# The even mixer in another order: attention pairs spread over inverse and chain, column groups at once, whole inverse steps

## Chip, core and metric

The kernel runs on one core of a Trainium2 chip. The metric is the time of one execution on the device in microseconds (us). Before the change the median of three runs is 1186.69 us (1185.93 to 1187.33).

## What is computed

One inference step of a two-layer trunk of width 1024, for 256 prompt tokens and 8 sample tokens that share the weights (264 columns in all). Each layer is a half-step SwiGLU, a mixer and another half-step SwiGLU, with a layer norm behind each. The even layer's mixer, the only part in question here, has 8 stick-breaking attention heads and 8 RWKV-7 heads, cut from the reference:

```python
def even_mixer(h, past_k, past_v, wkv0, shift0, prm, i):
    proj = h @ prm['w_in_even'][i]
    q, k, v = (heads(c) for c in jnp.split(proj[..., :SB_COLS], 3, axis=-1))
    ...
    pb = proj[..., SB_COLS:]
    pm = pb + prm['mu_shift'][i] * (prev - pb)
    r, kr, vr, wd, ad, gd = jnp.split(pm, RWKV_SPLITS, axis=-1)
    z_w = prm['w0'][i] + jnp.tanh(wd) @ prm['w_w2'][i]
    decay = jnp.exp(-jnp.exp(-jax.nn.softplus(-z_w) - 0.5))
    iclr = jax.nn.sigmoid(prm['a0'][i] + ad @ prm['w_a2'][i])
    gate = jax.nn.sigmoid(gd) @ prm['w_g2'][i]
    ...
    out = jnp.concatenate([o_sb, o_rwkv], axis=-1) @ prm['w_out_even'][i]
```

Attention takes z = q k'/8 + bias, and weights exp(log sigmoid(z) + the reversed running sum of log sigmoid(-z)) under the causal mask. The recurrence of a head keeps a 64x64 state s with s = s w - (s kk)(kk a)' + v k' and y = s r. The sample tokens attend to 256 past positions each, in a paged cache (16 pages of 128 positions).

## The kernel before

Activations lie with their channels on the partitions and the 264 tokens along the row. Weights stream from memory in the order of use, in chunks of eight 128x128 blocks (`Stream`); ScalarE rounds each chunk to `wh` (L197) and VectorE forms the rest `wl` (L198). `block` (L288 on) makes three matmuls of 264 columns of a weight block: `wh` with the high part of the activations, `wh` with the low one, `wl` with the high one (L295 to L297).

The even mixer (`_even`) first runs six blocks of columns at once into six PSUM banks (`FIRST_IN`: decay and learning-rate ranks, four blocks of `kr`, the gate's rank), on unnormalized activations, and then corrects and evicts them (`fix`, `in_proj`). `rwkv_first` makes the small decay and rate products (`pz`, `pa`), and `rwkv_prep` is a generator that prepares one pair of RWKV heads at a time on VectorE and ScalarE: the norm of the key (`pn`, `rsqrt`), the running decay (`cs`), and the scaled operands `ar`, `K`, `B`. Beside it run the blocks of `r` (`NEXT_IN`), then query, `vr`, key and value (`LAST_IN`). `proj` makes one such block of 128 columns from eight weight blocks into a bank `pi` of a group of two banks, and yields after every two.

The recurrence is solved in chunks of 64 tokens. `gram` makes masked products of the operands; `rwkv_inverse` inverts the unit-triangular matrices of 8 heads x 4 chunks (16 pairs) in six levels, each with the products `pP`, `pX` and `pXT`, each product in two halves of sixteen 64x64 matmuls on opposite quarters of the array; `rwkv_chain` then goes over the four chunks (`pW`, `pU`, `pS`, `pY`), and `rwkv_out` normalizes and gates.

All else is interleaved by generators: `_even` steps through the inverse and then the chain, and at each yield calls `next` on `side` (`other_half`: the remaining `proj` blocks, then attention, then the first half of the output projection `po`), on `tokens` (transposes), on `samples` (the paged attention of the sample tokens: keys on VectorE, then values as `pso` on TensorE) and on `states` (the samples' RWKV state on VectorE). `self.stage` tells how far `side` is. `behind` and `issue_after` fix parts of the order; the rest of each engine's order is set when the program is built. Banks lie in four groups, A (2), B (3), C (1) and D (2), that `banks` gives names.

Of the kernel before, what the change touches and what calls it, by code (L numbers as in the profile page):

```python
# [14 lines left out]
ALU = mybir.AluOpType  # L15
# [102 lines left out]
def even_order():  # L118
    o = [("w_in_even", 0, k, m) for k in range(KD) for m in FIRST_IN]
    o += [("w_in_even", 0, k, m) for m in NEXT_IN + LAST_IN for k in range(KD)]  # L120
# [98 lines left out]
class Trunk:  # L219
# [383 lines left out]
    def _even(self, ctx, ln_in, ln_out):  # L603
# [42 lines left out]
        ps = [self.ps([128, NO], f"raw{i}", t) for i, t in enumerate(("rk", "rk", "rk", "at", "at", "mm"))]  # L646
# [9 lines left out]
        self.rwkv_first(lora, hv)  # L656
        prep = self.rwkv_prep(hv, bone)
        next(prep)
        self.r_t = self.slot([128, 4, NT], "r_t")
        for mb in NEXT_IN:  # L660
            next(prep, None)
            for _ in self.proj(mb):
                pass
        for _ in prep:
            pass
# [4 lines left out]
        self.vtok = vv[:, 1]  # L670
        self.g2 = g2
# [16 lines left out]
        while self.stage < 3:  # L688
# [34 lines left out]
    def other_half(self, bone, sbb, idb, nmb):  # L723
# [3 lines left out]
        for mb in LAST_IN[:4]:  # L727
            yield from self.proj(mb)
        self.stage = 1
        for mb in LAST_IN[4:12]:  # L730
            yield from self.proj(mb)
            if mb == LAST_IN[7]:
                self.stage = 2
        nc.sync.dma_start(out=a["shift_out"], in_=self.sh_out)
        nc.sync.dma_start(out=a["kv_out"][:, 0], in_=self.k_t)
        self.stage = 3
# [42 lines left out]
    def rwkv_first(self, lora, hv):  # L779
# [3 lines left out]
        wa = self.tmp([128, NT], "wa")  # L783
        nc.scalar.activation(wa[0:64], self.wda[0:64], AF.Tanh)
        nc.vector.tensor_copy(wa[64:128], self.wda[64:128])
        nc.scalar.activation(self.gd, self.gd, AF.Tanh, scale=0.5)
        nc.vector.tensor_scalar(out=self.gd, in0=self.gd, scalar1=0.5, scalar2=0.5, op0=ALU.mult, op1=ALU.add)
# [8 lines left out]
        with self.tc.issue_after(last.ins):  # L796
            self.tables = self.load_exp_ln()

    def rsqrt(self, o, x):

        nc = self.nc
        with self.tc.issue_after(self.tables.ins):
            nc.scalar.activation(o, x, AF.Ln)
            nc.scalar.activation(o, o, AF.Exp, scale=-0.5)
        nc.vector.scalar_tensor_tensor(out=x, in0=x, scalar=-0.5, in1=o, op0=ALU.mult, op1=ALU.mult)
        nc.vector.tensor_tensor(out=x, in0=x, in1=o, op=ALU.mult)
        nc.vector.scalar_tensor_tensor(out=o, in0=x, scalar=1.5, in1=o, op0=ALU.add, op1=ALU.mult)

    def rwkv_prep(self, hv, bone):
# [14 lines left out]
        for m in range(4):  # L824
# [98 lines left out]
    def rwkv_inverse(self):  # L923
# [18 lines left out]
        for lv in range(6):  # L942
            lm = cst[:, None, C_LVL + 64 * lv:C_LVL + 64 * lv + 64].to_broadcast([128, 8, 64])
            P = {}
            for i, s in enumerate(S):
# [10 lines left out]
                yield  # L956
            if lv == 0:
                continue
            for i, s in enumerate(S):
                if lv < 5:  # L960
# [3 lines left out]
                    yield  # L964
# [3 lines left out]
                yield  # L968
# [108 lines left out]
    def attention(self, sbb, idb, nmb):  # L1077
# [8 lines left out]
        def scores(h):  # L1086
            m, H = h // 2, slice(h % 2 * 64, h % 2 * 64 + 64)
            z = self.ps([128, 384], "z", "at")
            mm(z[:, 0:256], lhsT=self.k_t[H, m, 0:128], rhs=self.q_t[H, m, 0:256], start=True, stop=False)
            mm(z[:, 0:256], lhsT=idb, rhs=nmb, start=False, stop=True)  # L1090
            mm(z[:, 256:384], lhsT=self.k_t[H, m, 128:256], rhs=self.q_t[H, m, 128:256], start=True, stop=False)
            mm(z[:, 256:384], lhsT=idb, rhs=nmb[:, 0:128], start=False, stop=True)
            zb[h], sp[h] = att("zb"), att("sp")
            nc.scalar.activation(zb[h], z, AF.Identity, bias=sbb[:, h:h + 1])
            self.softplus(sp[h], zb[h])
# [8 lines left out]
        def values(h):  # L1104
            m, H = h // 2, slice(h % 2 * 64, h % 2 * 64 + 64)
            po = self.ps([128, NP], "pov", "at")
            w = zb[h]
            mm(po[H, :], lhsT=vtok[:, 0, h * 64:h * 64 + 64], rhs=w[:, 0:256], start=True, stop=False)
            mm(po[H, 128:256], lhsT=vtok[:, 1, h * 64:h * 64 + 64], rhs=w[:, 256:384], start=False, stop=True)
            nc.scalar.copy(self.q_t[H, m, :NP], po[H])  # L1110
# [7 lines left out]
        for h in range(10):  # L1118
# [829 lines left out]
```

## Time and profile before

| | |
|---|---|
| median of three runs | 1186.69 us |
| the profiled execution: its own time | 1181.86 us |
| its span, first to last instruction | 1180.1 us |
| TensorE busy | 1126.4 us, 95% |
| VectorE busy | 881.6 us, 75% |
| ScalarE busy | 590.8 us, 50% |
| GpSimd busy | 176.8 us, 15% |
| mean granted TensorE clock | 0.982 |

Busy times are of one execution, and a busy TensorE is not TensorE at its peak: matmuls are pipelined and their ends are modelled. So the time of a piece of its queue is read from one start to the next. The page shows the share of each engine in 40 slices, and the waits, the timeline and the stretches of single engines come from the trace. The even mixer takes some 225 us, about from 235 to 460 us.

### The profile page before, as it was taken

How to read it: one execution, taken by the hardware profiler on the slowest of the kernel's cores; microseconds unless marked ns; L12 is line 12 of the kernel's file. 1: busy time of each engine (PE TensorE's matmuls, PEld its weight loads, DVE VectorE, ACT ScalarE, POOL GpSimd, SP SyncE). 2: the span in 40 equal slices, each digit the busy share in tenths (PEclk: the TensorE clock that was granted, in tenths of full speed). 3: DMA queues.
4: the chain of work that ended last, by engine and by line, in shares of the span. 5: the costliest groups of instructions: out<-in, count | busy, mean ns of one | idle time of the engine just before them, and what ended most of it. 6: DMA issues, size and time to landing. Idle time of an engine off the chain costs nothing. (4 is left out here: it accounts for less than half of the span.)

```text
span 1180.1 us, 26369 instructions
## 1 busy us (share of the span) xinstructions
PE 1126.4 (95%) x10711; PEld 1067.7 (90%) x10711; DVE 881.6 (75%) x1739; ACT 590.8 (50%) x1030; POOL 176.8 (15%) x296
## 2 busy tenths in 40 slices
PE   7999999979999998999999999999969999999996
PEld 6999999977986677999999999999958899999995
DVE  4999855889875769988876797675669699555564
ACT  4544544664245565744454564454463366444442
POOL 0000000364535314010110112100020002000000
PEclk9999999989999999999999999999979999999998
DMA  7755656624565314476775567665564253655651
GB/s 250 234 168 157 211 177 207 205 89 123 158 184 151 124 53 143 135 240 215 262 233 174 156 201 228 203 182 178 175 200 154 86 192 116 208 180 182 183 178 49
DMA packets 66122, 204.96 MB, mean 174 GB/s; under 512 B 13464, under 2 KB 16616, under 8 KB 65744
## 3 DMA queue, kind: packets, MB, share of 16 engines
q1 hardware_dynamic: 56400, 174.09, 47.4%
q0 software_dynamic: 6560, 23.27, 6.2%
q10 hardware_dynamic: 3040, 5.92, 1.6%
q8 instruction: 84, 1.38, 0.5%
q14 instruction: 38, 0.31, 0.1%
HBM read 192.22 MB, written 10.86 MB: 172 GB/s over the span
## 5 line engine op out<-in xcount | busy, mean ns | idle before, releaser
L198 DVE TENSOR_TENSOR wl<-raw,wh 128x1024 fp32r<-128x1024 f32 (+2 forms) x317 | 388.5, 1227 | 184.0 <-ACT wh L197 180.9
L197 ACT CAST wh<-raw 128x1024 fp32r<-128x1024 f32 (+2 forms) x317 | 329.9, 1041 | 344.5 <-issue 100.0
L295 PE MATMUL pd<-hh,wh 128*128 128x264 f32 x704 | 200.8, 285 | 0.0
L297 PE MATMUL pd<-hh,wl 128*128 128x264 f32 x704 | 200.7, 285 | 0.0
L296 PE MATMUL pd<-hl,wh 128*128 128x264 f32 x704 | 199.1, 283 | 0.0
L295 PE MATMUL pg<-xh,wh 128*128 128x264 f32 x648 | 184.8, 285 | 3.3 <-DVE fixc L467 1.8
L297 PE MATMUL pg<-xh,wl 128*128 128x264 f32 x648 | 184.4, 285 | 1.6 <-DVE wl L198 1.5
L296 PE MATMUL pg<-xl,wh 128*128 128x264 f32 x648 | 183.6, 284 | 0.0
L297 PE MATMUL pu<-xh,wl 128*128 128x264 f32 x608 | 173.2, 285 | 2.0 <-DVE wl L198 1.9
L295 PE MATMUL pu<-xh,wh 128*128 128x264 f32 x608 | 172.9, 284 | 0.0
L296 PE MATMUL pu<-xl,wh 128*128 128x264 f32 x608 | 172.7, 284 | 0.0
L295 PEld LDWEIGHTS pd<-hh,wh 128*128 128x128 f32 x704 | 132.4, 188 | 0.6
L297 PEld LDWEIGHTS pd<-hh,wl 128*128 128x128 f32 x704 | 132.6, 188 | 0.2
L296 PEld LDWEIGHTS pd<-hl,wh 128*128 128x128 f32 x704 | 132.4, 188 | 0.0
L295 PEld LDWEIGHTS pg<-xh,wh 128*128 128x128 f32 x648 | 122.4, 189 | 4.2 <-ACT xh L451 2.0
L297 PEld LDWEIGHTS pg<-xh,wl 128*128 128x128 f32 x648 | 121.8, 188 | 2.7 <-DVE wl L198 2.7
L296 PEld LDWEIGHTS pg<-xl,wh 128*128 128x128 f32 x648 | 122.5, 189 | 0.0
L297 PEld LDWEIGHTS pu<-xh,wl 128*128 128x128 f32 x608 | 114.3, 188 | 3.0 <-DVE wl L198 2.9
L296 PEld LDWEIGHTS pu<-xl,wh 128*128 128x128 f32 x608 | 115.0, 189 | 0.0
L295 PEld LDWEIGHTS pu<-xh,wh 128*128 128x128 f32 x608 | 114.9, 189 | 0.0
L295 PE MATMUL raw<-rh,wh 128*128 128x266 f32 x192 | 56.7, 295 | 3.8 <-DVE r L346 3.7
L498 ACT CAST hh<-h 128x264 fp32r<-128x264 f32 x79 | 32.2, 409 | 55.6 <-DVE h L497 55.4
(559 smaller groups left out, 2214.6 us busy)
## 6 DMA issues: line engine op xcount, KB each, us to landing
raw<-in_w SPq DMA_DIRECT2D x308, 512.0 KB, 3.7
raw<-in_w SPq DMA_DIRECT2D x7, 384.0 KB, 5.5
gxd<-gc SPq DMA_DIRECT2D x8, 256.0 KB, 2.7
qb<-qd POOLq DMA_DIRECT2D x8, 256.0 KB, 4.5
FT<-wd POOLq DMA_DIRECT2D x8, 256.0 KB, 5.4
bF<-in_bF POOLq DMA_DIRECT2D x8, 256.0 KB, 4.4
rot<-rotd ACTq DMA_DIRECT2D x5, 384.0 KB, 5.2
rotd<-T POOLq DMA_DIRECT2D x2, 768.0 KB
```

The lines of the kernel that those rows point to most:

```text
L197: nc.scalar.copy(wh[:, :w], raw[:, :w])
L198: nc.vector.tensor_tensor(out=wl[:, :w], in0=raw[:, :w], in1=wh[:, :w], op=ALU.subtract)
L295: mm(ps, lhsT=wh, rhs=xh, start=start, stop=False)
L296: mm(ps, lhsT=wh, rhs=xl, start=False, stop=False)
L297: self.last_mm = mm(ps, lhsT=wl, rhs=xh, start=False, stop=stop)
L498: self.last = [nc.scalar.copy(hh[:, m, :], h), self.last_mm]
```

## The change

Query blocks come right behind the first six (`SOON_IN`) and between the receptance blocks; key, value and `vr` blocks are taken by `attention` itself, which now goes by pairs of heads and starts with the inverse. A pair's scores use both halves of the rows, its values both halves of the columns. The samples' values run four pages at a time on four groups of 32 columns, so the pages are loaded four at a time. `rwkv_inverse` yields once per product and no longer per half. In the preparation five operations go from VectorE to ScalarE or GpSimd, and `rsqrt` has one VectorE operation less and a square on ScalarE. The table load for exponential and logarithm stands behind the last hyperbolic tangent, and `softplus` behind that load. The core of the diff:

```diff
-FIRST_IN = [WDA, WKR, WKR + 1, WKR + 2, WKR + 3, WGD]
-NEXT_IN = [WR + i for i in range(4)]
-LAST_IN = list(range(4)) + [WVR + i for i in range(4)] + list(range(4, 12))
+FIRST_IN = [WDA, WGD, WKR, WKR + 1, WKR + 2, WKR + 3]
+SOON_IN = [WQ, WQ + 1]
+NEXT_IN = [WR, WQ + 2, WR + 1, WQ + 3, WR + 2, WR + 3]
+LAST_IN = [WK, WV, WVR, WVR + 1, WK + 1, WV + 1, WVR + 2, WVR + 3, WK + 2, WV + 2, WK + 3, WV + 3]
...
-        ps = [self.ps([128, NO], f"raw{i}", t) for i, t in enumerate(("rk", "rk", "rk", "at", "at", "mm"))]
+        ps = [self.ps([128, NO], f"raw{i}", t) for i, t in enumerate(("rk", "rk", "rk", "at", "at", "sa"))]
...
         for i, _ in enumerate(self.rwkv_inverse()):
-            if self.stage < 3:
+            for _ in range(1 + i % 2):
                 next(side)
-            if i < BURST:
-                next(side)
-            if i >= 4 and i % 3 == 2:
+            if i >= 4:
                 next(tokens, None)
-            if i > 5 and (i % 2 or i > 24):
                 next(samples, None)
...
         for i, _ in enumerate(self.rwkv_chain(bone)):
             next(gate, None)
-            next(side, None)
-            next(side, None)
+            for _ in range(1 + i % 2):
+                next(side, None)
...
-        nc.vector.scalar_tensor_tensor(out=x, in0=x, scalar=-0.5, in1=o, op0=ALU.mult, op1=ALU.mult)
-        nc.vector.tensor_tensor(out=x, in0=x, in1=o, op=ALU.mult)
+            nc.scalar.activation(s, o, AF.Square)
+        nc.vector.scalar_tensor_tensor(out=x, in0=x, scalar=-0.5, in1=s, op0=ALU.mult, op1=ALU.mult)
...
-            nc.vector.tensor_scalar(out=lw, in0=lw, scalar1=1.0, scalar2=None, op0=ALU.add)
+            nc.scalar.activation(lw, lw, AF.Copy, bias=1.0)
...
-            nc.vector.tensor_scalar(out=kki, in0=ti, scalar1=0.5, scalar2=0.5, op0=ALU.mult, op1=ALU.add)
+            nc.scalar.activation(kki, ti, AF.Copy, scale=0.5, bias=0.5)
...
-            nc.vector.tensor_scalar(out=kf, in0=ti, scalar1=hv[:, 8 + m:9 + m], scalar2=hv[:, 12 + m:13 + m],
-                                    op0=ALU.mult, op1=ALU.add)
+            nc.scalar.activation(kf, ti, AF.Identity, scale=hv[:, 8 + m:9 + m], bias=hv[:, 12 + m:13 + m])
...
+        def scores(m):
+            z = [self.ps([128, 384], "z", "at") for _ in range(2)]
+            for o, k, q, n in ((slice(0, 256), slice(0, 128), slice(0, 256), nmb),
+                               (slice(256, 384), slice(128, 256), slice(128, 256), nmb[:, 0:128])):
+                for i in range(2):
+                    H = slice(64 * i, 64 * i + 64)
+                    mm(z[i][:, o], lhsT=self.k_t[H, m, k], rhs=self.q_t[H, m, q], start=True, stop=False)
+                for i in range(2):
+                    mm(z[i][:, o], lhsT=idb, rhs=n, start=False, stop=True)
...
+        def values(m):
             po = self.ps([128, NP], "pov", "at")
+            for w in range(2):
+                for i in range(2):
+                    h = 2 * m + i
+                    mm(po[64 * i:64 * i + 64, 128 * w:256], lhsT=vtok[:, w, h * 64:h * 64 + 64],
+                       rhs=zb[h][:, (0, 256)[w]:(256, 384)[w]], start=w == 0, stop=w == 1)
...
+        turns = [[8 * g + 2 * i + p for i in range(4)] for g in range(2) for p in range(2)]
+        for e in turns[0]:
             load(e)
         for g in range(2):
+            po = self.ps([128, 512], "pso", "sa")
+            for p in range(2):
+                for _ in range(4):
+                    yield
                 with self.tc.issue_after(self.anchor.ins):
+                    for i, e in enumerate(turns[2 * g + p]):
+                        mm(po[32 * i:32 * i + 32, :], lhsT=w[:, e * 8:e * 8 + 32], rhs=vp[e], start=p == 0, stop=p == 1)
+                if p == 0:
+                    for e in turns[2 * g + 1]:
+                        load(e)
```

How the order of the instructions moves is shown at three places. The first is VectorE in the opening, the preparation of the first pair of RWKV heads (`pn` is the norm, `t0` and `t1` the steps of `rsqrt`, `cs` the running decay, `wl` the splits of weight chunks). Before, and then with the change:

```order
L832 TENSOR_SCALAR t0_3379<-pn_3381 128x264
L805 SCALAR_TENSOR_TENSOR t0_3379<-t0_3379,t1_3383 128x264
L806 TENSOR_TENSOR t0_3379<-t0_3379,t1_3383 128x264
L807 SCALAR_TENSOR_TENSOR t1_3383<-t0_3379,t1_3383 128x264
L198 TENSOR_TENSOR wl_3554<-raw_3551,wh_3553 128x1024
L835 SCALAR_TENSOR_TENSOR kk_3390<-kr_t_3030,vec_76,t1_3383 128x264
L839 SCALAR_TENSOR_TENSOR cs_3393<-cst_75,lw_3343 128x264
L847 TENSOR_SCALAR kki_3399<-ti_3344 128x264
L198 TENSOR_TENSOR wl_3624<-raw_3621,wh_3623 128x1024
L848 TENSOR_TENSOR kki_3399<-kki_3399,kk_3390 128x264
L850 TENSOR_SCALAR ti_3344<-ti_3344,hv_3019 128x264
L853 TENSOR_TENSOR ar_3374<-kk_3390,E1_3370 128x4x64
```

```order
L826 TENSOR_SCALAR t0_3445<-pn_3447 128x264
L199 TENSOR_TENSOR wl_3481<-raw_3478,wh_3480 128x1024
L800 SCALAR_TENSOR_TENSOR t0_3445<-t0_3445,t2_3451 128x264
L801 SCALAR_TENSOR_TENSOR t1_3449<-t0_3445,t1_3449 128x264
L829 SCALAR_TENSOR_TENSOR kk_3457<-kr_t_3030,vec_76,t1_3449 128x264
L833 SCALAR_TENSOR_TENSOR cs_3460<-cst_75,lw_3407 128x264
L199 TENSOR_TENSOR wl_3552<-raw_3549,wh_3551 128x1024
L842 TENSOR_TENSOR kki_3466<-kki_3466,kk_3457 128x264
L846 TENSOR_TENSOR ar_3440<-kk_3457,E1_3436 128x4x64
```

One step of `rsqrt` and the two affine steps ahead of `kki` and `ti` are gone from VectorE; the addition to `lw` (L837 before) too.

The second place is TensorE at the scores (`z` the scores, `idb` and `nmb` the mask). Before, one head between weight blocks and the chain, and with the change the first pair, ahead of the first `gram`:

```order
L297 MATMUL pi_4740<-xh_3226,wl_4344 128x264
L1089 MATMUL z_5028<-qk_3667 128x256
L1090 LDWEIGHTS idb_3023
L1090 MATMUL z_5028<-nmb_3025,idb_3023 128x256
L1091 MATMUL z_5028<-qk_3667 128x128
L1092 LDWEIGHTS idb_3023
L1092 MATMUL z_5028<-nmb_3025,idb_3023 128x128
L1003 MATMUL pS_5047<-VT_4892,KT_4606 64x64 x5
```

```order
L1086 MATMUL z_3866<-qk_3338 128x256
L1086 MATMUL z_3867<-qk_3338 128x256
L1088 LDWEIGHTS idb_3023
L1088 MATMUL z_3866<-nmb_3025,idb_3023 128x256
L1088 LDWEIGHTS idb_3023
L1088 MATMUL z_3867<-nmb_3025,idb_3023 128x256
L1086 MATMUL z_3866<-qk_3338 128x128
L1086 MATMUL z_3867<-qk_3338 128x128
```

The two heads' matmuls of one kind now stand next to each other, and the first pair stands ahead of the inverse.

The third place is the end of the mixer, TensorE just ahead of the output projection (`pso` the samples' values, `pst` their transposition, `pov` the heads' values, `po` the output projection). Before, and with the change:

```order
L1209 MATMUL pso<-vp,sw 32x512
L1099 MATMUL pcs<-att,cst 128x384
L1100 MATMUL pcs<-att,cst 128x128
L996 MATMUL pU<-Wn,XT 64x64 x3
L1108 MATMUL pov<-att,vv 64x256
L1109 MATMUL pov<-att,vv 64x128
L996 MATMUL pU<-Wn,XT 64x64 x5
L1003 MATMUL pS<-VT,KT 64x64 x2
L1108 MATMUL pov<-att,vv 64x256
L1109 MATMUL pov<-att,vv 64x128
L1003 MATMUL pS<-VT,KT 64x64 x5
L1221 MATMUL pst<-cst,soc 128x128
```

```order
L1296 MATMUL psy<-cst,sys 32x32 x2
L1224 MATMUL pso<-vp,sw 32x512 x2
L1108 MATMUL pov<-att,vv 64x256 x2
L1108 MATMUL pov<-att,vv 64x128
L1224 MATMUL pso<-vp,sw 32x512
L1108 MATMUL pov<-att,vv 64x128
L1296 MATMUL psy<-cst,sys 32x32 x2
L1043 MATMUL pgm<-YT,cst 128x288
L1224 MATMUL pso<-vp,sw 32x512
L1049 MATMUL pgv<-t_5755,cst 128x288
L1237 MATMUL pst<-cst,soc 128x128
L296 MATMUL po<-xh,wh 128x264 x4
```

Before, the last `pso` stood ahead of the last chain step, and `pst` inside it; now the last four `pso` come behind that step, one by one, and `pst` is the last matmul ahead of `po`.

## Rows read from the trace of the kernel before

**Rows 1.** The page, part 1: busy us, share of the span, instructions.

```profile
PE 1126.4 (95%) x10711; PEld 1067.7 (90%) x10711; DVE 881.6 (75%) x1739; ACT 590.8 (50%) x1030; POOL 176.8 (15%) x296
```

**Rows 2.** TensorE's waits from 235 to 460 us: total, times, longest.

```profile
PE pi L295 <- DVE fixt L469: 3.8, 1, 3.8
PE pi L295 <- ACT pb L590: 2.6, 1, 2.6
PE pP L940 <- DVE ss L947: 2.3, 2, 1.5
```

**Rows 3.** Stretches: length, busy us (count) of PE, PEld, DVE, ACT, POOL; clock; DMA.

```profile
240.00:250.00 10.00, 7.75 (x29) 6.72 (x30) 8.36 (x19) 6.54 (x15) 7.08 (x19) 0.66 0.17 53
260.00:270.00 10.00, 9.03 (x60) 8.97 (x61) 8.98 (x19) 5.16 (x13) 6.86 (x18) 0.83 0.36 107
296.00:356.00 60.00, 59.88 (x1122) 52.98 (x1117) 49.24 (x78) 22.33 (x46) 26.95 (x36) 1.00 0.59 175
```

**Rows 4.** Timeline of TensorE in the inverse: start us, us, instruction, count.

```profile
297.14 1.15 PE L940 MATMUL pP<-X,ss 64*64 64x64 f32 x32
298.22 0.39 PE L295 MATMUL pi<-xh,wh 128*128 128x264 f32 x1
298.45 0.28 PE L296 MATMUL pi<-xl,wh 128*128 128x264 f32 x1
298.57 0.28 PE L297 MATMUL pi<-xh,wl 128*128 128x264 f32 x1
...
299.14 1.15 PE L940 MATMUL pP<-X,ss 64*64 64x64 f32 x32
...
344.75 1.15 PE L940 MATMUL pX<-st,XT 64*64 64x64 f32 x32
345.73 1.10 PE L940 MATMUL pXT<-XT,st 64*64 64x64 f32 x32
```

**Rows 5.** Groups of VectorE from 235 to 296 us: busy us, mean ns, idle before.

```profile
L806 DVE TENSOR_TENSOR t<-t,t 128x264 f32<-128x264 f32 x4 | 1.7, 430 | 0.1
```

**Rows 6.** Timeline of TensorE at the samples' values (two records to a matmul).

```profile
363.35 1.90 PE L1209 MATMUL pso<-vp,sw 128*32 128x512 f32 x6
...
380.73 1.91 PE L1209 MATMUL pso<-vp,sw 128*32 128x512 f32 x4
...
426.73 1.04 PE L1209 MATMUL pso<-vp,sw 128*32 128x512 f32 x2
```

**Rows 7.** Timeline of TensorE at one head's scores and another's values.

```profile
386.58 0.70 PE L1089 MATMUL z<-qk 64*128 64x256 f32 x2
387.21 0.28 PE L1090 MATMUL z<-nmb,idb 128*128 128x256 bf16 x1
387.43 0.49 PE L1091 MATMUL z<-qk 64*128 64x128 f32 x2
387.84 0.23 PE L1092 MATMUL z<-nmb,idb 128*128 128x128 bf16 x1
...
388.93 0.65 PE L1108 MATMUL pov<-att,vv 128*64 128x256 f32 x2
389.41 0.38 PE L1109 MATMUL pov<-att,vv 128*64 128x128 f32 x2
389.72 0.27 PE L1003 MATMUL pS<-VT,KT 64*64 64x64 f32 x1
```

**Rows 8.** The tile `vp`: durations in ns (least, median, most), and landing.

```profile
L1197 POOL DMA_INDIRECT vp<-in_cache_v,idx x16: 944/972/1432, 353.1 to 410.2; - x16
...
DMA to landing us min/median/max: 3.4/3.7/4.6
```

**Rows 9.** Timeline of VectorE at the samples' sums.

```profile
427.81 0.69 DVE L1214 TENSOR_TENSOR pv<-pso,cst 128x512 f32<-128x512 f32 x1 [0.71 <-PE pso L1209]
...
429.68 1.04 DVE L1216 TENSOR_REDUCE soc<-pv 128x64 f32<-128x512 f32 x1
...
432.19 0.73 DVE L1226 COPY qk<-pst 64x16 f32<-64x16 f32 x4 [1.13 <-PE pst L1221]
```

More of the change, by code (lines that the diff above doesn't have):

```diff
@@ L119, in even_order @@
     o = [("w_in_even", 0, k, m) for k in range(KD) for m in FIRST_IN]
[L120 removed]
+    o += [("w_in_even", 0, k, m) for m in SOON_IN + NEXT_IN + LAST_IN for k in range(KD)]
     o += [("w_out_even", 0, k, m) for m in range(KD) for k in range(4)]
@@ L670, in _even @@
         self.vtok = vv[:, 1]
+        for mb in SOON_IN:
+            for _ in self.proj(mb):
+                pass
+        self.rwkv_first(lora, hv)
+        prep = self.rwkv_prep(hv, bone)
+        next(prep)
+        self.r_t = self.slot([128, 4, NT], "r_t")
+        for i, mb in enumerate(NEXT_IN):
+            if i < 4:
+                next(prep)
+            for _ in self.proj(mb):
+                pass
+        for _ in prep:
+            pass
         self.g2 = g2
@@ L796, in rwkv_first @@
         with self.tc.issue_after(last.ins):
+            last = nc.scalar.activation(self.gd, self.gd, AF.Tanh, scale=0.5)
+        nc.gpsimd.tensor_scalar(out=self.gd, in0=self.gd, scalar1=0.5, scalar2=0.5, op0=ALU.mult, op1=ALU.add)
+        with self.tc.issue_after(last.ins):
             self.tables = self.load_exp_ln()
@@ L1084, in attention @@
         att = lambda name: self.tw([128, 384], "att", bufs=6)
[L1086 to L1095, printed above, removed]
+        def scores(m):
[9 more added lines that the diff above has]
+                h = 2 * m + i
+                zb[h], sp[h] = att("zb"), att("sp")
+                nc.scalar.activation(zb[h], z[i], AF.Identity, bias=sbb[:, h:h + 1])
+            for i in range(2):
+                self.softplus(sp[2 * m + i], zb[2 * m + i])
         def weights(h):
@@ L1102, in weights @@
             nc.scalar.activation(zb[h], zb[h], AF.Exp)
-        def values(h):
-            m, H = h // 2, slice(h % 2 * 64, h % 2 * 64 + 64)
+        def values(m):
             po = self.ps([128, NP], "pov", "at")
[L1107 to L1110, printed above, removed]
+            for w in range(2):
+                for i in range(2):
+                    h = 2 * m + i
+                    mm(po[64 * i:64 * i + 64, 128 * w:256], lhsT=vtok[:, w, h * 64:h * 64 + 64],
+                       rhs=zb[h][:, (0, 256)[w]:(256, 384)[w]], start=w == 0, stop=w == 1)
+            nc.scalar.copy(self.q_t[:, m, :NP], po)
         def tokens(m):
@@ L1116, in tokens, with blocks @@
             nc.scalar.copy(vtok[:, :, m * 128:m * 128 + 128], ps)
-        for h in range(10):
-            m = h // 2
-            if h in (0, 2, 4, 6):
-                yield from self.proj(WV + m)
-            if h < 8:
-                scores(h)
-            if h in (0, 2, 4, 6):
-                tokens(m)
-            if h == 6:
-                nc.sync.dma_start(out=self.a["kv_out"][:, 1], in_=self.v_t)
+        left = list(LAST_IN)
+        def blocks(n):
+            for _ in range(n):
+                yield from self.proj(left.pop(0))
+        for m in range(4):
+            yield from blocks((2, 2, 2, 0)[m])
+            if m == 0:
+                self.stage = 1
+            scores(m)
+            yield
+            tokens(m)
+            yield from blocks((1, 1, 1, 0)[m])
+            if m == 3:
+                yield
+            for i in range(2):
+                weights(2 * m + i)
+            yield
+            yield from blocks((1, 1, 1, 0)[m])
+            if m == 1:
+                self.stage = 2
+                nc.sync.dma_start(out=self.a["shift_out"], in_=self.sh_out)
+            if m == 2:
+                for i, t in enumerate((self.k_t, self.v_t)):
+                    nc.sync.dma_start(out=self.a["kv_out"][:, i], in_=t)
                 self.new_h()
                 self.oh, self.ol = self.xh, self.xl
-            if 1 <= h < 9:
-                weights(h - 1)
-            if h >= 2:
-                values(h - 2)
+            values(m)
             yield
@@ L1198, in load @@
                                          in_offset=bass.IndirectOffsetOnAxis(ap=idx[:, e:e + 1], axis=0))
[L1200 removed]
+        turns = [[8 * g + 2 * i + p for i in range(4)] for g in range(2) for p in range(2)]
+        for e in turns[0]:
             load(e)
         for g in range(2):
[L1203 to L1212 removed]
+            po = self.ps([128, 512], "pso", "sa")
+            for p in range(2):
+                for _ in range(4):
+                    yield
+                with self.tc.issue_after(self.anchor.ins):
+                    for i, e in enumerate(turns[2 * g + p]):
[3 more added lines that the diff above has]
+                        load(e)
+            if g == 0:
+                for e in turns[2]:
+                    load(e)
             t = self.page([128, 512], "pv")
```

56 lines of the change are left out of this document (12 added, 44 removed).

## The prediction

> **What bounds the kernel now.** Read first the page's busy shares: TensorE is busy for 1126.4 of 1180.1 us [rows 1], so only work that leaves TensorE's queue, or time in which it stands still, can be won. The even mixer lies between about 235 us (first `pi` block) and 460 us. Read there the stretches, then TensorE's waits. Two kinds of loss are to be seen. In the opening TensorE stands still: 3.8, 2.6 and 2.3 us, 8.7 us in all [rows 2], and the mean granted clock is 0.66 and 0.83 in two stretches of 10 us [rows 3], which is 6.8 and 3.4 us at the lower of its two levels (1.2 for 2.4 GHz). From 296 us on it never waits and the clock is at 1.00 [rows 3]: that part is as long as the instructions in TensorE's queue. There, the time of a piece is read from start to start. Outside this stretch the change touches nothing; I take the rest as it is.
>
> **How the pieces of TensorE's queue add up.** A block of six matmuls between two groups of the inverse takes 0.92 us (298.22 to 299.14), and the starts in it are 0.12 us apart, so 0.2 us of it is the change from one shape to the other. A group of sixteen 64x64 matmuls takes 1.08 us after a block (297.14 to 298.22), and 0.98 us when the next group follows at once [rows 4]. As a check I added up everything in the queue this way for 296 to 460 us, and it came to the length of that stretch within 1%.
>
> **The change, part by part.** The matmuls are the same ones, 672 of them weight blocks; what changes is their order.
>
> - *Opening.* Two query blocks (48 matmuls, 5.8 us) come ahead of the decay and gate work, query blocks alternate with receptance blocks, and the sixth first accumulator lies in a bank of its own, so that the third block no longer waits for its eviction. Both long waits of [rows 2] had this cause: the block behind found its bank not yet read, once because the read stood behind five others on VectorE, once because ScalarE's read needed a buffer that VectorE gives back. Along with it, 16 of VectorE's instructions in the preparation (four lines of four, of which the costliest takes 0.43 us each [rows 5]; some 6 us in all) go to ScalarE or vanish. They stood in the queue that TensorE waited for. ScalarE is busy for 6.5 and 5.2 of 10 us there [rows 3] and takes them in its gaps; without gaps, four of them would make each pair 1.7 us later. To be won at most: 8.7 us of waits and (6.8 - 2.25 + 3.4 - 0.97) / 2 = 3.5 us of slow clock (what TensorE stood still inside those two stretches taken off), 12.2 us. I leave 1.5 us for new short waits, since a preparation of a pair takes VectorE about ten instructions of 0.4 to 0.7 us, partly overlapped, some 4 us, and one or two weight splits, while TensorE gets 48 to 72 matmuls, 6 to 9 us, between two of them. Bounds: 0, and 9 us, as long as now.
> - *Sample values.* Sixteen matmuls of 32 columns stand in twelve places now, nine single ones of 1.0 us and three runs of 1.9 us [rows 6], 14.7 us. Four on four column groups come together now: three turns at 1.0 us, and the last turn in three places, 6.0 us. That gains **8.7 us**. That column groups run side by side is to be seen already: three matmuls of which two lie on different groups (363.35) take 1.90 us, as long as two on one group (380.73) [rows 6]. Four at once no row shows; if only two ran together, each turn but the last takes 1.9 and it is 6.0, if none, 0.
> - *Attention in pairs.* The values of a head take 0.48 and 0.31 us [rows 7]; on two column groups a pair takes what one head takes: 4 x 0.79 = **3.2 us**. The scores of a head take 0.63 and 0.41 us on 64 rows, with two short bf16 matmuls behind them; the pair uses both halves of the rows and two banks: 4 x 1.04 = **4.2 us**. Nearest rows are the 64x64 groups, whose pairs on both halves run at 0.98 us for sixteen. In series it is 0 for each.
> - *Whole inverse steps.* Thirty groups of sixteen become fifteen of thirty-two: 2.03 instead of 2 x 1.08 us, **1.9 us**. Weight blocks stand in 38 pieces instead of 51 (counted in the order): 13 x 0.2 = **2.6 us**.
> - *Table change, `softplus` held behind the table load.* Three table loads stand in this stretch before and after. Nothing; ScalarE is busy for 22.3 of the 60 us from 296 us on [rows 3].
> - *New waits.* The end of the mixer is the place. The last four pages of the value cache are fetched only when the third turn has read the buffers; GpSimd takes 0.97 us to issue each, and 3.7 us pass to landing [rows 8]. The second is there 0.1 + 0.97 + 3.7 = 4.8 us later; TensorE has until then 15 `pY` matmuls (0.9 us at the pace of [rows 4]) and two `pcs` of two matmuls (387.84 to 388.93, 1.0 us each [rows 7]), so it waits about 2 us (and the same time covers the last pair's `softplus`). Then the sums of the samples: 0.69 us of multiplication and 1.04 us of reduction [rows 9] follow the last `pso`, the transposition `pst`, four copies of 0.73 us together [rows 9], and a split on ScalarE, before the first `po` can start. All this was hidden under the chain; now only one `pgv` (some 0.5 us, as a `pov` of 256 columns [rows 7]) lies over it, so 3 us more. With 1 us for a clock that may fall after it, the end costs **6 us** (bounds 2 and 12). The first chain step follows the last token transposition without the group that lay between, 0.5 us. The second turn's pages, issued behind the first's reads, 1 us (0 to 4). For VectorE, which is 82% busy in 296 to 356 us [rows 3], I add 1 us (0 to 8).
>
> One rule weighed against a row. The sample values of [rows 6] on two column groups overlap. The Trainium skill, "TensorE: Matmul & The Clock Gate", section "Part 3: Packing small matmuls", says that a weight load runs beside a matmul only when its row group differs; column groups share all rows. By it the pages and the values of attention would go one after another and the two terms of 8.7 and 3.2 us would be nothing; the row at 363.35 speaks against this for 32 columns, and the same page gives a gain for column groups.
>
> **Sum.** 12.2 + 8.7 + 3.2 + 4.2 + 1.9 + 2.6 = 32.8 us won; 1.5 + 6 + 0.5 + 1 + 1 = 10 us lost; 22.8 us net. The profiled execution took 1181.86 us for a span of 1180.1, so it would become 1159. The median of the runs shown is 4.8 us above it, and I take that to stay: 1186.7 - 22.8 = **1164 us**.
>
> **Rivals.**
> - *Column groups in series.* The terms of 8.7 and 3.2 us fall away: 1164 + 11.9 = 1175.9. For it: no row shows four at once, nor 64 columns. Against it: [rows 6]. One in ten. The rule above would have it so.
> - *VectorE or ScalarE late.* The stretch shrinks from 225 to some 200 us while VectorE loses only 6 of its work, so its share rises. If each of the fourteen steps of the inverse waits 0.5 us, and the states of the chain the same again, 1164 + 10 = 1174. For it: 82% and in-order queues. Against it: VectorE was as busy per step before, with no wait. Fourteen in a hundred.
> - *The end stays covered.* If pages and sums arrive in time and nothing new waits, 10 us come back but for 3: 1157. One in ten.
> - *Slower: the inverse falls to the low clock.* A step now reads what the step just before it wrote, both halves of it, with one piece of weight blocks (0.92 us) and the other half's group (1.0 us) as cover. If an eviction takes longer than these 1.9 us step after step, because ScalarE has a weight split of 1.05 us ahead of it, TensorE waits in each step and, as in [rows 3] at 240 us, is granted the lower clock. Half of 60 us of work at half speed is 30 us more, and 14 x 0.5 us of waits: 1164 + 37 = 1201. Against it: ScalarE is only 37% busy there. Four in a hundred; it decides from an eviction of 1.9 us on.
>
> **Numbers.** Forecast 0.62, then 0.10, 0.14, 0.10 and 0.04. A measurement of this kernel can tell 0.2% (2.4 us) from no change. All but the last are faster by more, 0.96; I take 0.02 off for a rival of these that goes twice as far as reckoned, which would be no change: 0.94, 0.02 and 0.04. The range reaches up to the first two rivals, and so takes in any one of the bounds above, not two at once; below, it takes in the covered end: 1155 to 1176.
>
> **What would show it.** In the opening: no wait of TensorE over 1 us and a granted clock of 1.00 from 240 to 290 us. Four `pso` starting within 0.1 us of each other and about 1 us until the next instruction; a pair of `z` and of `pov` within the time of one head. No waits in the inverse. At the end, waits of TensorE for `vp` or `pso`'s sums, some 5 us together, just ahead of `po`. It would be wrong if `pso` took 3 to 4 us a turn, or if TensorE waited for the groups' evictions in the inverse.

## The result, and the profile after

| | before | with the change |
|---|---|---|
| median, first measurement (4 runs each) | 1186.31 us | 1171.37 us (1169.02 to 1175.06) |
| ratio and its 95% interval | | 0.9881 [0.9856, 0.9907] |
| ratio, second and third measurement | | 0.9905 [0.9886, 0.9924]; 0.9873 [0.985, 0.9897] |
| profiled execution, its own time | 1181.86 us | 1175.06 us |

The change is 12 to 16 us faster in three measurements. The forecast was 1164 us, 22.8 us less than before; the time lies inside its range, and the sign was right, but some 8 us of the gain are missing.

The page of the changed kernel, part 1, answers to [rows 1]:

```profile
PE 1113.8 (95%) x10711; PEld 1062.4 (91%) x10711; DVE 875.1 (75%) x1721; ACT 592.7 (51%) x1043; POOL 179.0 (15%) x297
```

TensorE has the same number of instructions and 12.6 us less of busy time. Its waits from 235 to 460 us, against [rows 2]; total, times, longest:

```profile
PE pn L824 <- ACT t L822: 3.9, 3, 2.0
PE pst L1237 <- DVE soc L1234: 1.5, 1, 1.5
PE po L296 <- ACT xh L1068: 1.5, 1, 1.5
PE pP L933 <- DVE X L956: 1.2, 1, 1.2
PE pz L781 <- ACT ti L785: 1.2, 1, 1.2
...
PE pz L781 <- POOL pb L590: 0.9, 1, 0.9
PE pgm L1043 <- issue: 0.9, 1, 0.9
PE pbn L876 <- DVE bon L877: 0.9, 1, 0.9
PE pso L1224 <- DMA vp<-in_cache_v,idx: 0.8, 1, 0.8
PE z L1086 <- DVE bon L1030: 0.7, 1, 0.7
```

Before, the long waits stood in the opening and there was none from 296 us on. Now the two longest are gone, and some twenty short ones stand in all parts of the mixer (the ten largest groups in the mixer are shown). The stretches, against [rows 3] (length, busy us of PE, PEld, DVE, ACT, POOL; clock; DMA):

```profile
240.00:250.00 10.00, 7.90 (x47) 6.62 (x46) 7.79 (x15) 8.59 (x20) 6.76 (x18) 1.00 0.29 97
250.00:260.00 10.00, 9.48 (x76) 9.21 (x76) 7.55 (x13) 9.18 (x22) 4.75 (x12) 1.00 0.37 113
260.00:270.00 10.00, 8.68 (x70) 8.19 (x69) 8.83 (x16) 7.74 (x18) 4.28 (x8) 1.00 0.61 193
275.00:285.00 10.00, 7.95 (x48) 5.18 (x48) 7.86 (x15) 7.29 (x19) 2.32 (x5) 0.66 0.44 139
296.00:356.00 60.00, 57.24 (x1122) 51.25 (x1118) 44.46 (x71) 22.61 (x47) 26.74 (x36) 0.97 0.50 147
```

The stretch from 250 us in the kernel before, which [rows 3] leave out:

```profile
250.00:260.00 10.00, 8.38 (x65) 8.01 (x63) 7.89 (x16) 7.51 (x14) 3.40 (x8) 1.00 0.37 113
```

The clock holds at 240 and 260 us, where it was 0.66 and 0.83, and falls at 277 us instead, right behind a wait for `pn`. ScalarE, which was busy for 6.5, 7.5 and 5.2 of 10 us from 240, 250 and 260 us on, is busy for 8.6, 9.2 and 7.7. The inverse has a clock of 0.97 and TensorE stands still in it.

What the pairs and the turns did, from the timeline of TensorE, against [rows 6, 7] (start, us, instruction, count of records, wait before):

```profile
304.94 0.87 PE L1108 MATMUL pov<-att,vv 128*64 128x256 f32 x8
305.74 1.09 PE L909 MATMUL gram<-ar,K 64*64 64x128 f32 x16
...
377.67 0.70 PE L1086 MATMUL z<-qk 64*128 64x256 f32 x2
379.02 0.69 PE L1086 MATMUL z<-qk 64*128 64x256 f32 x2 [0.66 <-DVE bon L1030]
...
383.79 1.06 PE L1224 MATMUL pso<-vp,sw 128*32 128x512 f32 x8
384.78 0.68 PE L990 MATMUL pU<-Wn,XT 64*64 64x64 f32 x16
...
392.98 1.18 PE L1224 MATMUL pso<-vp,sw 128*32 128x512 f32 x4
395.00 1.70 PE L1224 MATMUL pso<-vp,sw 128*32 128x512 f32 x4 [0.85 <-DMA vp<-in_cache_v,idx]
396.64 0.70 PE L1043 MATMUL pgm<-YT,cst 128*128 128x256 f32 x2
...
422.00 1.04 PE L1224 MATMUL pso<-vp,sw 128*32 128x512 f32 x2
423.40 1.04 PE L1224 MATMUL pso<-vp,sw 128*32 128x512 f32 x2 [0.35 <-issue]
```

Four `pso` take 0.99 us (383.79 to 384.78) and a pair's values 0.80 us, as one head's did. The second turn came apart at its pages (1.2 us, a wait, 1.6 us), and the last one stands as four single matmuls of about 1.0 us (the first two are shown). The scores of a pair stand whole and at the high clock nowhere in this profile: here, at 377.67 us, the second head waits for its bank, since a pair takes both banks of group D. How long a whole pair takes is to be seen in one of the kernels below (square_and_sums), on TensorE:

```profile
276.35 0.70 PE L1094 MATMUL z<-qk 64*128 64x256 f32 x4 [2.26 <-ACT qk L586]
...
277.94 1.09 PE L917 MATMUL gram<-ar,B 64*64 64x128 f32 x16
```

From 276.35 to 277.94 that is 1.59 us for both heads. One head took 1.33 us before, from 386.58 us [rows 7] to the next instruction of TensorE:

```profile
387.91 0.86 PE L1099 MATMUL pcs<-att,cst 128*128 128x384 f32 x2
```

A whole pair saves 2 x 1.33 - 1.59 = 1.07 us, and 1.04 were reckoned. So column and row groups give what was reckoned, where the matmuls stand together.

To set the terms of the sum against this, the time from each start to the next in TensorE's queue was added up by tile from the first `pi` to the first `raw` behind `po`, the waits that the profile names taken off. The second profile is that of changed_again below, the same kernel once more:

| us | before | changed, first profile | changed, second profile |
|---|---|---|---|
| first `pi` to first `raw` | 225.5 | 222.7 | 216.4 |
| waits | 10.0 | 18.6 | 17.6 |
| queue without waits | 215.5 | 204.1 | 198.8 |
| of it weight blocks `pi` | 70.2 | 66.3 | 65.0 |
| groups of the inverse | 32.0 | 31.9 | 31.2 |
| `pso` | 14.3 | 8.8 | 8.6 |
| `z` | 10.9 | 9.5 | 8.8 |
| `pov` | 6.3 | 3.6 | 3.6 |

The two profiles of one kernel differ by 6.3 us here. Their waits are alike; in the first the clock falls at three places in between (277, 315 and 380 us), in the second at one (278 us). The mean clock of the mixer is 0.97 and 0.99, which by the trace costs 6.8 and 1.7 us: 5.1 of the 6.3 us.

### The profile page after: what moved, and what is told of

It is laid out like the page before. It is cut to its first block, busy times and chain, and to the rows that moved or that the text cites. A ratio compares the mean times of both kernels' runs of the same rounds, so it can differ in the third digit from the quotient of the medians.

```text
span 1173.3 us, 26359 instructions
## 1 busy us (share of the span) xinstructions
PE 1113.8 (95%) x10711; PEld 1062.4 (91%) x10711; DVE 875.1 (75%) x1721; ACT 592.7 (51%) x1043; POOL 179.0 (15%) x297
```

## The experiments

The kernels of one measurement share a chip. The kernel before took 1179.0 us on the chip of the first four and 1186.7 and 1187.2 us on those of the next two fours, so times are compared within a measurement, and ratios to the kernel before across them. The changed kernel itself was not among the first four, which are compared with it by their ratios alone.

**The square ahead (square_early).** On ScalarE the square that `pn` needs stands behind the exponentials of the pair before, though it needs only `kr`. The timeline of ScalarE of the changed kernel:

```profile
267.27 0.60 ACT L844 ACTIVATE ti<-ti,hv 128x264 f32<-128x264 f32 x1
267.78 0.50 ACT L822 ACTIVATE t<-kr_t,vec 128x264 f32<-128x264 f32 x1
```

`pn` starts at 268.33 us, behind that last row, after a wait of 1.32 us.

```diff
+        def ahead(m):
+            square.append(self.tw([128, NT], "sq", tag="att", bufs=6))
+            nc.scalar.activation(square[-1], self.kr_t[:, m, :], AF.Square, scale=self.v(V_KK, m))
...
-            nc.scalar.activation(sq, kr, AF.Square, scale=self.v(V_KK, m))
+            sq = square.pop(0)
...
+            if m < 3:
+                ahead(m + 1)
             nc.scalar.activation(lw, lw, AF.Copy, bias=1.0)
```

> The changed kernel, with the square of the next pair's key issued on ScalarE ahead of the current pair's exponentials (buffers of its own). Theory (the opening's loss is the order on ScalarE): TensorE's three waits for it ahead of pn, 3.9 us in the changed kernel's trace, go, and with them the lower clock granted from 277 to 284 us, some 3 us: 4 to 7 us faster than the changed kernel, 19 to 22 us below the kernel before. Rival (a pair's preparation as a whole is late, on VectorE too): the waits reappear at the first gram matmuls, which read the pair's ar, and the time is within 1 us of the changed kernel, 14 to 16 us below the kernel before.

1168.26 us, ratio 0.9906 [0.9878, 0.9935]: no more than the changed kernel. Its waits from 235 to 285 us:

```profile
PE z L1094 <- ACT qk L586: 2.3, 1, 2.3
PE pz L781 <- ACT ti L785: 1.2, 1, 1.2
PE pi L296 <- ACT pb L591: 1.1, 1, 1.1
```

The waits for `pn` are gone, and 3.4 us stand ahead of `z` and `pi`, for evictions on the same ScalarE. The place was right, the price was not: the wait moved, as the rival had it, but not to the `gram` matmuls that the rival named; it moved to other readers of ScalarE's queue.

**Sums first (sums_first, sums_first_again).** At the end of the mixer the first product `pv` of the samples' values comes 20 us behind the second turn's `pso`. The timeline of VectorE of the changed kernel:

```profile
414.84 0.68 DVE L1289 TENSOR_TENSOR ss<-st,svx 128x512 f32<-128x512 f32 x1
...
416.44 0.68 DVE L1232 TENSOR_TENSOR pv<-pso,cst 128x512 f32<-128x512 f32 x1
```

The third turn's pages take four of five page buffers, and `svx` holds the fifth until the row at 414.84. `pv` waits for that buffer, and the third turn for the bank that `pv` reads: it starts at 417.17 us, 20 us behind the second, though its pages were issued from 394 us on.

```diff
-            if g == 0:
-                for e in turns[2]:
-                    load(e)
             t = self.page([128, 512], "pv")
...
             nc.vector.tensor_reduce(out=oc[:, g, :], ...
+            if g == 0:
+                for e in turns[2]:
+                    load(e)
             yield
```

> The changed kernel, with the product pv of the first four samples' values written ahead of the loads of the third turn's pages, so that it takes the free page buffer. Theory (the first pv stands at 416.4 us, 20 us after its pso, because the loads took every page buffer but the one that holds svx until 415.5, and the third turn's pso needs pv's bank): the third turn moves up by some 10 us, pst comes ahead of the last gated normalization, the waits ahead of pst and po (3.0 us) and the gaps between the last single pso go: 3 to 5 us faster than the changed kernel, 18 to 20 us below the kernel before. Rival (the end is set by the last RWKV rows or by the last pair's attention, and the sums lie beside them): po starts as late as now, within 1 us of the changed kernel.

> The kernel that forms the samples' first sums ahead of the third turn's loads, now beside the changed kernel. Theory (the end of the mixer, from the last pY to the first raw, is some 6 us shorter, as in its first profile: 30.1 against 36.2 us, and nothing else changes): 4 to 7 us faster than the changed kernel. Rival (what the end gains is given back, by work that was moved into the chain, or by the clock): 0 to 3 us faster.

The mechanism holds in both profiles: the first `pv` starts at 388.4 us in the first of them, `pst` stands ahead of the last `pgv`, and from the last `pY` to the first `raw` it is 30.1 and 29.2 us where the changed kernel has 36.2 (37.8 in its profile beside the second). The time does not follow: the ratio is 0.9882 [0.9856, 0.9908], and beside the changed kernel it is 1172.67 against 1171.52 us, 0.9882 [0.9862, 0.9901] against 0.9873. In its second measurement the gain was given back in the chain: from the first `pW` to the last `pY` it took 57.6 us in the first profile, 64.7 in the second, and 57.3 in the changed kernel beside that. The waits of the second there:

```profile
PE pU L990 <- ACT Wn L986: 2.2, 1, 2.2
PE pso L1224 <- DMA vp<-in_cache_v,idx: 2.0, 1, 2.0
```

and its stretches (length, busy us of TensorE, clock, DMA):

```profile
405.00:410.00 5.00, 2.78 (x47) 1.00 0.81 249
410.00:415.00 5.00, 5.00 (x61) 0.68 0.22 86
415.00:420.00 5.00, 5.00 (x54) 0.64 0.00 0
```

Behind the wait of 2.2 us the clock falls, and some 7 us run at the lower level: (5 x 0.32 + 5 x 0.36) x 2 = 6.8 us, 3.4 us lost. ScalarE's timeline shows why `Wn` was late:

```profile
405.99 0.41 ACT L1053 ACTIVATE t<-t 128x256 f32<-128x256 f32 x1
409.29 0.38 ACT L986 ACTIVATE Wn<-pW 128x256 f32<-128x256 f32 x1 [2.88 <-remote]
```

ScalarE paused for 2.9 us for something that the profile only calls remote; the matmuls `pW` that `Wn` reads were through when TensorE's next tile started, at 406.23 us. In its first measurement no such pause stands in the kernel's profile. The two other kernels with sums first that were measured beside it have it too, ahead of `Wn`, 2.9 us each. The changed kernel has a pause of 2.9 to 3.0 us in all three of its profiles, ahead of an exponential of `att`, where TensorE does not wait for it.

**Both, and the decay ahead (square_and_sums, square_and_sums_again, decay_ahead).** The first two join the edits. The last kernel also writes a pair's `lw`, `cs`, `E` and `En` ahead of `pn` and `rsqrt`:

```diff
+            nc.scalar.activation(lw, lw, AF.Copy, bias=1.0)
+            cs = self.tmp([128, NT], "cs")
+            nc.vector.tensor_tensor_scan(out=cs, data0=scan_mask, data1=lw, ...)
...
             sq = square.pop(0)
             pn = self.ps([128, NT], "pn", "rk")
...
-            nc.scalar.activation(lw, lw, AF.Copy, bias=1.0)
-            cs = self.tmp([128, NT], "cs")
-            nc.vector.tensor_tensor_scan(out=cs, data0=scan_mask, data1=lw, ...)
...
```

> Both of the other two edits in one kernel. If both theories hold and the two places are independent: 7 to 12 us faster than the changed kernel, 22 to 27 us below the kernel before, and the sum of the two single gains within 2 us. If both rivals hold: 14 to 16 us below the kernel before.

> Sums first and the square of the next pair's key early, beside the changed kernel. The early square alone had moved the wait (2.3 us ahead of z for the key block's eviction in place of 3.6 to 3.9 us ahead of pn), so it is worth 1 to 3 us on top of the sums: 6 to 10 us faster than the changed kernel, and 1 to 3 us faster than the sums alone. Rival (the opening is not shorter at all, the time only stands in another wait): within 1 us of the sums alone.

> As the kernel with early square and sums first, and in each pair of the preparation the running decay and its exponentials (lw, cs, E, En) are written ahead of the inverse root of the key's norm. Theory (E waits 2.0 to 3.2 us on ScalarE for cs, which stands on VectorE behind the inverse root, and the key block's eviction stands behind E): z's wait of 2.3 us shrinks to under 1 us, and it is 1 to 3 us faster than early square and sums alone. Rival (the order within a pair does not matter, since VectorE works through the whole pair in any case): within 1 us of it, with the wait still ahead of z or of a gram.

0.9859 [0.9829, 0.989], 0.9855 [0.9837, 0.9874] and 0.9856 [0.9838, 0.9874]; beside the changed kernel 1170.87 and 1170.92 against 1171.52 us. So the gains do not add up, no kernel beside the changed one is faster than it by more than the measurement tells, and the order inside a pair changes nothing: with the decay ahead, `z` still waits for the key block's eviction.

```profile
PE z L1094 <- ACT qk L586: 2.1, 1, 2.1
```

**Half steps (half_steps).** The inverse yields after each half again.

```diff
                     P[i] = self.tw([128, 8, 64], "st", bufs=2)
                     nc.scalar.copy(P[i], ps)
+                if i == 0:
+                    yield
             yield
```

with the `yield` of `pX` and `pXT` moved into the loop over the halves, and `next(side)`, tokens and samples shared out so that a whole step gets as much as now.

> The changed kernel, with the inverse going on by half steps again (16 matmuls, then what stands between, then the other 16), everything else as changed. By the sum of the prediction: 1.9 us for the split groups and up to 2.6 us for more pieces of weight blocks, so up to 4.5 us slower than the changed kernel, 10 to 13 us below the kernel before. Rival (whole steps are what makes TensorE wait for VectorE in the inverse, 3.5 us of waits and some 1.8 us of lower clock behind them): these go, and it is 0 to 3 us faster than the changed kernel.

1177.85 us (10 runs), ratio 0.999 [0.9968, 1.0012]: nearly all of the change's gain is gone, more than the 4.5 us of the sum, and the rival fails. Its waits in the mixer add up to 18.0 us, as with whole steps, though those of the inverse are 1.4 us for 2.2 and 3.1. Weight blocks take 67.3 us (65.0 in the second profile of the changed kernel), groups of the inverse 31.6 (31.2). More is due to the clock: the queue without waits is 206.9 us long, 8.1 more than in that profile, and the mean clock of the mixer is 0.96 for 0.99, which by the trace costs 8.5 us for 1.7. A wait for `pbn` that was 0.9 us is now longer,

```profile
PE pbn L880 <- DVE bon L881: 2.3, 2, 2.1
```

and behind it the clock is low for some 10 us:

```profile
355.00:360.00 5.00, 2.72 (x11) 0.95 0.58 164
360.00:365.00 5.00, 4.54 (x20) 0.50 0.02 7
365.00:370.00 5.00, 5.00 (x34) 0.53 0.00 0
```

**The changed kernel again (changed_again, changed_control).**

> The changed kernel itself, beside the next three on one chip. Theory (part of the missing gain in its first profile was the clock, granted low four times between 275 and 465 us, and that differs from one execution to the next): the mixer, from the first pi to the first raw behind po, is 216 to 220 us long here, not 222.7, with the same waits of TensorE within 1 us; the ratio to the kernel before is again 0.986 to 0.991. Rival (the mixer is always that long and the rest of the gain lies elsewhere): 222 to 223 us, with low clock in the same four places.

> The changed kernel once more, as the mark for the next three on the same chip. By its two measurements so far (ratios 0.9881 and 0.9905 to the kernel before): 0.988 to 0.991, 10 to 14 us below the kernel before. Its profile should show the three waits for pn (3.6 to 3.9 us in all), the waits ahead of pst and po (3.0 us), and the mixer 216 to 223 us long, the longer the more often the clock is low in it.

1174.61 against 1186.69 us and 1171.52 against 1187.18 us. The mixer is 216.4 and 218.6 us long in their profiles, and the waits for `pn` are 3.8 and 3.6 us: the theory holds, the clock is what differs between executions. The four runs of changed_again had 1171.84 us at a mean clock of 0.984, 1173.58 at 0.983, 1175.65 at 0.982 and 1177.35 at 0.980. Time times clock is 1153.1 to 1154.5 in all four, so nearly all of the spread of 5.5 us is clock. This product compares kernels with the clock taken out; between executions of one kernel it moves by up to 7 us, so its means are given below.

**One column group (one_column_group).**

```diff
-mm(po[32 * i:32 * i + 32, :], lhsT=w[...], rhs=vp[e], start=p == 0, stop=p == 1)
+mm(po[0:32, :], lhsT=w[...], rhs=vp[e], start=p == 0 and i == 0, stop=p == 1 and i == 3)
```

The sums behind it then take in these 32 rows alone; the kernel leaves out the results of the single pages.

> The changed kernel, with the four pages of a turn going into the same 32 columns, one after another into one sum (the samples' results are left wrong: the sums of four pages stand in the place of one, and the other three rows of results are zero). Theory (matmuls on different column groups run side by side, and that alone made a turn of four as short as one): a turn takes 3.8 to 4.0 us in place of 1.0, 11 to 12 us slower than the changed kernel. Rival (standing together is what made them short, as consecutive groups of 64x64 are shorter): 1.0 to 1.3 us a turn, the time unchanged. Between them: turns that wait for pages or for sums anyway take some of it up, 6 to 10 us.

Its first turn on TensorE:

```profile
379.88 3.62 PE L1225 MATMUL pso<-vp,sw 128*32 128x512 f32 x8
383.43 0.68 PE L990 MATMUL pU<-Wn,XT 64*64 64x64 f32 x16
```

3.55 us where four column groups take 0.99: the groups run side by side, and standing together is not what made them short. All `pso` take 15.7 us of the queue, 7.0 more than in the changed kernel, since turns that came apart had little to lose. The median is 1175.11 against 1174.61 us all the same (ratio 0.9897 [0.988, 0.9914]). The profiled execution, at 1180.6 us, is the slowest of four, with a mean clock of 0.981; the other three, at 1173.6 to 1176.4 us, had 0.984 to 0.986 where the changed kernel had 0.980 to 0.984. Time times clock is 1157.3 on the mean against 1153.8, 3.5 us more. Why the clock was granted higher there is open.

**No query ahead, preparation on VectorE (no_query_ahead, preparation_on_vector).**

```diff
-SOON_IN = [WQ, WQ + 1]
-NEXT_IN = [WR, WQ + 2, WR + 1, WQ + 3, WR + 2, WR + 3]
+SOON_IN = []
+NEXT_IN = [WR, WQ, WR + 1, WQ + 1, WR + 2, WQ + 2, WR + 3, WQ + 3]
```

> The changed kernel, with no query block ahead of the decay products: the list of blocks that come soon is empty, and receptance and query blocks alternate behind, four of each. Theory of the prediction (the two query blocks are the cover for the evictions that the decay products wait for): 5.8 us of cover go, and TensorE stands still for 4 to 6 us more ahead of pz: 4 to 8 us slower than the changed kernel, with a lower clock there. Rival (the opening is as long as VectorE's and ScalarE's preparation in any case): the two blocks are cover for the preparation behind, the waits for pn (3.9 us) go, and it is within 2 us of the changed kernel.

1178.1 us, ratio 0.992 [0.9903, 0.9936], against 1174.61 us: 3.5 us slower, with overlapping intervals. From the first `pi` to the first `gram` it is 45.2 us, against 44.8 in the changed kernel beside it. The waits ahead of `pz` did not grow, nor did those for `pn` go (4.1 us in two). A new wait of 2.1 us stands ahead of `pvt`, for ScalarE's `att`. Neither theory stands: the two blocks ahead are no cover that `pz` needs. Nor do the two old waits ahead of `pi` come back without them, so these blocks are not what took them away; the bank for the sixth accumulator and the order of the first six blocks remain, and no run takes those apart.

```diff
-            nc.scalar.activation(kki, ti, AF.Copy, scale=0.5, bias=0.5)
+            nc.vector.tensor_scalar(out=kki, in0=ti, scalar1=0.5, scalar2=0.5, op0=ALU.mult, op1=ALU.add)
```

and the same for `lw` and `kf`.

> The changed kernel, with the three steps of the preparation that went to ScalarE (the addition to lw, kki's and kf's affine steps, four of each) back on VectorE. If ScalarE's queue is what pn waits for: ScalarE has some 5 us less ahead of the squares, the three waits for pn shrink from 3.9 to below 2 us, 2 to 4 us faster than the changed kernel. Rival (VectorE is the bound of the preparation): its 12 instructions of 0.42 us put the pair's end back, pn's or gram's waits grow by 2 to 5 us in all, and it is 2 to 5 us slower.

1174.42 us, ratio 0.9908 [0.9885, 0.993]: no difference in time. Its mean clock is higher, though, 0.985 against 0.982, and time times clock is 1157.4 us, 3.6 above the changed kernel; without query ahead it is 1157.2. With the clock taken out, then, these three steps on ScalarE seem worth some 3 us, which the time does not show. The waits for `pn` fall to 2.2 us, and others come up, from 235 to 296 us:

```profile
PE pn L824 <- ACT t L822: 2.2, 1, 2.2
...
PE pi L296 <- ACT pb L591: 1.1, 1, 1.1
...
PE gram L909 <- DVE ar L854: 0.8, 1, 0.8
```

## Why the prediction was right, and where 8 us went

- *Opening: 12.2 us won, 1.5 lost.* This is the step that failed. Of the old waits of 8.7 us all but 0.6 went, but 6.0 us of new ones came (`pn` 3.9, `pz` 1.2 and 0.9) where "I leave 1.5 us for new short waits" stood; that was inside the bounds of 0 and 9. The low clock did not go either, it moved: 6.8 us of it at 275 to 285 us, (1 - 0.66) x 10 x 2, where [rows 3] had 6.8 and 3.4. In the second profile it is 3.4 us there. So the waits gave 8.7 - 6.6 = 2.1 us and not 7.2, the clock at most 1.7 in the first profile and 3.4 in the second, where 3.5 stood: some 5 to 7 us short. Of the 8.7 us, 2.3 were waits of the inverse's first `pP` for VectorE, for which the prediction names no reason to go; the 0.6 us that stayed are theirs. The reason that I gave, that ScalarE takes the moved work in its gaps, was read from how busy it was before; it had 3.5, 2.5 and 4.8 us of gaps in 10 from 240, 250 and 260 us on, and the change left 1.4, 0.8 and 2.3. With the moved work taken back, or the square ahead, the waits only change their place. That speaks for the preparation on both engines together, and not for one order in it, as what TensorE waits for.
- *Sample values: 8.7 us.* The mechanism is right, 0.99 us a turn, and 3.55 on one group. The size was 5.6 us: the second turn waits for its pages and takes 2.8 us, the last one four times 1.0. Reckoned were 1.0 and 3.0. By the reading of the Trainium skill ("TensorE: Matmul & The Clock Gate", section "Part 3: Packing small matmuls") that was weighed there, a turn would have been as long on four column groups as on one. The two rows, 0.99 and 3.55 us, contradict that. The same section of the Trainium skill gives a gain of 2.38 times for three matmuls packed by columns. The rows agree with such a gain: 3.55 / 0.99 = 3.6 times for four.
- *Attention.* Values 2.8 us for 3.2. Scores 1.3 to 2.1 us for 4.2: a pair takes 1.59 us, as reckoned, where it stands whole at the high clock, but the first pair ran at the low clock behind `pn` and the others were split, by waits for the second bank or by other work.
- *Whole steps and pieces: 1.9 and 2.6 us.* The groups gave 0.1 to 0.8 us, the blocks 3.8 to 5.2, which takes in what the clock gave back in the opening. Undone, these two cost about the whole gain of time, but that is not their worth: with the clock taken out, the half-step kernel is 4.6 us below the kernel before (time times clock 1155.3 against 1159.9 on the mean), the changed kernel 9.6 and 8.4 us. The 4 to 5 us between them are what the two terms say; the rest is the low clock of the half-step kernel, 0.981 on the mean, which they did not have.
- *The end: 6 us.* `pst`, `po` and `pgm` wait 3.4 us, and the single `pso` lie open. The size was about right, the cause only in part: not the last pages were late first, but the third turn itself, for a buffer. With that taken away the end is 6 to 9 us shorter and the time the same, which I had not reckoned with.
- *VectorE: 1 us.* In the inverse TensorE waits 3.1 us (`pP` 1.2, 0.7 and 0.6, `pX` and `pXT` 0.3 each), and 1.6 us ahead of the chain (`pbn`, `tok`). That is the rival of the late engines, at about half its price.

Sorted like the table, the forecast had 20.6 + 3.5 - 1 = 23.1 us less of queue, clock taken in, and -8.7 + 1.5 + 5 + 0.5 + 1 + 1 = 0.3 us more of waits. The second profile has 16.7 us less of queue and 7.6 us more of waits, 9.1 us; the first, with a lower clock, 2.8. So in the mixer, where the forecast looked for all of its 22.8 us, less than half came, and that the time lies in the range is in part luck. Of the 6.8 us between the two profiled executions of the first measurement, 4.0 lie behind the mixer, where the change touches nothing and the mean clock was 0.982 for 0.978. The rest of the measured 12 to 16 us is that the profile of before was one of its faster executions (1181.86 us for a median of 1186.31), while the changed kernel's two lie 3.7 us above and 2.8 below their medians: the 4.8 us of which I wrote "I take that to stay" did not stay.

Time times mean clock tells the same without the choice of a profile. In the second and third measurement it is 1163.4 and 1163.5 us on the mean before and 1153.8 and 1155.1 with the change: 9.6 and 8.4 us less, where the forecast had 22.8 - 3.5 + 1 = 20.3 us without its clock terms. The other 2.5 and 7.3 us of the measured gains are a higher mean clock (0.981 to 0.982, and 0.980 to 0.985); what raised it, no run here shows.

## What to carry to other kernels

Where the queue of the busiest engine is shortened, the engines that feed it come up: reckon the new waits from the gaps that these have left after the move, and not from those that they had before. A wait that is taken away gives nothing if the next instruction waits for the same engine's queue; look at the reader after the next. A buffer pool shared by short and long holders is followed through all its holders: here a buffer held for the states of one part kept a sum, a bank and a whole turn of another part waiting for 20 us.

## What was not expected of the hardware

- Removing standstills did not raise the granted clock. Beside each other, the changed kernel had a mean clock of 0.985 over five runs and the kernel with sums first 0.982. Time times clock fell from 1155.1 to 1151.4 us, 3.7 us, and the time not at all: the clock gave back what the order had won.
- Whether the clock falls behind a wait is not fixed by its length. The same wait ahead of the same `pn` stands in the changed kernel's first profile and in the second of the kernel with sums first:

```profile
277.20 1.23 PE L824 MATMUL pn<-t,cst 128*128 128x264 f32 x2 [2.05 <-ACT t L822]
...
276.30 0.71 PE L824 MATMUL pn<-t,cst 128*128 128x264 f32 x2 [2.05 <-ACT t L822]
```

  Behind the first the clock fell for 7 us; behind the other it stayed at 1.00, as it was from 235 to 387 us. In the kernel with both edits it stayed at 1.00 from 235 to 435 us in its first profile in spite of a wait of 2.3 us ahead of `z`.
- The kernels with sums first have a pause of 2.9 us on ScalarE ahead of `Wn` in one measurement and none in the other, in which the kernel before was 8 us faster too. What ScalarE waits for stays open.
